# Up-projection weights of a conv-FFN: store fewer split operands, split three of seven anew in each chunk

## The chip, the cores and the metric

The kernel runs on one core of one Trainium2 chip. TensorE multiplies; VectorE, ScalarE and GpSimd (POOL in the profile) prepare operands and take results out of PSUM; SyncE (SP) issues nearly all DMAs from one in-order queue. The metric is device time in microseconds, the median of the runs.

## The reference

One layer of a hybrid decoder: a mixing sub-layer (dilated window attention and gated linear attention) and a feed-forward sub-layer, for 2048 prompt tokens and 64 sample tokens. The change is in the second half, the feed-forward part, and in what leads to it:

```python
def conv_ffn(xn, conv_buf, w_up, conv_w, conv_b, w_down):
    T = xn.shape[1]
    up = xn @ w_up
    g, u = jnp.split(up, 2, axis=-1)
    gp = jnp.concatenate([conv_buf.astype(g.dtype), g], axis=1)
    c = conv_b + sum(conv_w[j] * gp[:, j:j + T] for j in range(CONV_W))
    h = jax.nn.gelu(c, approximate=False) * u
    return h @ w_down, gp[:, T:]
...
    x = x + rmsnorm(mixed, g_post_mix)
    f, conv_new = conv_ffn(rmsnorm(x, g_pre_ffn), conv_buf, w_up, conv_w, conv_b, w_down)
    x = x + rmsnorm(f, g_post_ffn)
```

The model width is 1024, the hidden width 2816 (22 tiles of 128), all in float32.

## The kernel before, in words

**Precision.** Every float32 operand is split into a high part (ScalarE rounds it, line 68) and a low part (operand minus high part, on GpSimd or VectorE, line 71; the argument "p" or "v" chooses). A product then takes three matmuls: high x high, high x low, low x high.

**Chunks.** The 2112 tokens are cut into four chunks of 528, each of two halves of 264. `tail` first runs the output projection (`wo`, with its inputs from `wo_x` and its normalisation in `post`) for all four chunks, and then `ffn` four times. `ffn` walks over pairs of hidden tiles, 11 pairs a chunk, in the groups of `FG` (sizes in tiles). For each pair it computes the gate product, the convolution and gelu, then the up product (`strassen` with z = 0 and z = 1), multiplies the two and splits the result into hh and hl. After a group, `down` multiplies the group's hidden tiles with the down weights and adds to `acc`, eight output tiles m.

**Seven products.** `strassen` computes a 2 x 2 block product (two hidden tiles by two token halves, over the two halves of the model width) with seven products instead of eight. Each product is 12 matmuls of 264 columns: 4 model tiles by 3 parts. Its seven weight operands come from the generator `wsrc`, and the seven input operands from `ffn_x`. Results leave PSUM by ScalarE copies (lines 1381, 1383) and VectorE adds (line 1379), in between further products that add to the same bank.

**Where the operands come from.** In chunk 0, `wsrc` loads two raw weight tiles of 512 KB (`wraw`, tile wr), forms three sums on VectorE (four operations, lines 1363 to 1366), splits all seven operands, low parts alternately on GpSimd and VectorE, and stores all seven in DRAM (d_wst, line 1372). Chunks 1 to 3 load the seven, 512 KB each (line 1357). The down weights go the same way: raw and split in chunk 0, stored in d_wdst (line 1407), loaded in the later chunks (line 1402).

**Order and buffers.** The order of work on each engine and on the DMA queue comes from a scheduler with a timeline of its own, starting from the order of the program text. Split weights pass through a ring of eight slots ("w") in the feed-forward part. Raw weights have two buffers, raw input tiles five. The final step of a chunk (`final`, normalisation and output) is a generator `pend`, which the next chunk advances by four steps after each `strassen`, and drains at the end of its first group (in chunk 0, of its second).

```python
        for i, src in enumerate((g0[:, lo], g0[:, hi], t3[:, 1], g1[:, lo], t3[:, 0], t3[:, 2], g1[:, hi])):
            t = self.slot("w", [128, 2, 512], F32R, "ws")
            t4 = t.rearrange("p a (k c) -> p a k c", k=4)
            self.split(t4[:, 0], t4[:, 1], src, "pvpvpvp"[i])
            yield t4
            nc.sync.dma_start(wt[i], t.bitcast(F32))
```

Of the kernel before, what the change touches and what calls it, by code (L numbers as in the profile page):

```python
# [18 lines left out]
KT = 8  # L19
# [8 lines left out]
H = 264  # L28
FCH = tuple((2 * H * c, H, H) for c in range(4))
FG = (2, 4, 4, 4, 4, 4)  # L30

# [5 lines left out]
class Layer:  # L37
# [1131 lines left out]
    def raw(self):  # L1169
        return self.xpool.tile([128, 2 * H], F32, name=self.n("br"), tag="raw", bufs=5)  # L1170

    def wraw(self, src, nk=8):
        raw = self.xpool.tile([128, 8, 128], F32, name=self.n("wr"), tag="wr", bufs=2)
        self.nc.sync.dma_start(raw[:, :nk], src.rearrange("p (k c) -> p k c", k=nk))
        return raw
# [24 lines left out]
    def tail(self):  # L1200
        nc, a = self.nc, self.a
        with ExitStack() as ctx:
            self.xpool = self.pool(ctx, "tx", side="right")
            self.gk = "h"
            self.slots, self.scnt = {}, {}
            self.bx = [self.xpool.tile([128, 2 * H], F32, name=self.n("bx"), tag="px", bufs=3) for _ in range(3)]
            p = self.npool = self.pool(ctx, "tn")
            self.psum = self.pool(ctx, "tps", bass.MemoryType.PSUM)
            posts = []
            with ExitStack() as c1:  # L1210
                self.spool = self.pool(c1, "tw")
                self.ring("w", 4, 12)
                self.ring("hl", 8, 16)
                self.wow = []
                for _ in self.wo_x(0):
                    pass
                for c in range(4):
                    nxt = self.wo_x(c + 1) if c < 3 else iter(())
# [24 lines left out]
            for _ in pend:  # L1243
                pass

    def wo_x(self, c):
# [5 lines left out]
        for k in self.WORD:  # L1252
# [37 lines left out]
    def post(self, c, mot, ssq):  # L1290
# [7 lines left out]
        for m in range(KT):  # L1298
            r = self.bx.pop(0) if self.bx else self.xpool.tile([128, w], F32, name=self.n("bx"), tag="px", bufs=3)
            nc.sync.dma_start(r, a["xn"][:, m, t0:t0 + w])  # L1300
# [14 lines left out]
    def ffn_x(self, c):  # L1315
# [35 lines left out]
    def wsrc(self, c, f, z):  # L1351
        nc, a = self.nc, self.a
        wt = a["wst"][f // 2, z]
        if c:
            for i in range(7):
                t = self.slot("w", [128, 2, 512], F32R, "ws")
                nc.sync.dma_start(t.bitcast(F32), wt[i])
                yield t.rearrange("p a (k c) -> p a k c", k=4)
            return
        g0, g1 = (self.wraw(a["wu"][2 * (f + j) + z]) for j in range(2))  # L1360
        t3 = self.spool.tile([128, 3, 4, 128], F32, name=self.n("wt"), tag="wt", bufs=1)
        lo, hi = slice(0, 4), slice(4, 8)
        nc.vector.tensor_tensor(t3[:, 0], g0[:, lo], g1[:, lo], op=ALU.subtract)
        nc.vector.tensor_tensor(g1[:, lo], g1[:, lo], g1[:, hi], op=ALU.add)
        nc.vector.tensor_tensor(t3[:, 1], g1[:, lo], g0[:, lo], op=ALU.subtract)
        nc.vector.tensor_tensor(t3[:, 2], g0[:, hi], t3[:, 1], op=ALU.subtract)
        for i, src in enumerate((g0[:, lo], g0[:, hi], t3[:, 1], g1[:, lo], t3[:, 0], t3[:, 2], g1[:, hi])):
# [4 lines left out]
            nc.sync.dma_start(wt[i], t.bitcast(F32))  # L1372

    def strassen(self, c, f, z, xs, o11, o12, o21, o22):
# [3 lines left out]
        p1, u2, u4 = (self.spool.tile([128, H], F32, name=self.n(n), tag=n, bufs=2) for n in ("p1", "u2", "u4"))  # L1378
        add = lambda o, x, y: nc.vector.tensor_tensor(o, x, y[:, :H], op=ALU.add)
        for i, (bank, new, ev) in enumerate((  # L1380
# [8 lines left out]
            for k in range(4):  # L1389
                xh, xl = xs[self.PROD[i]][k]  # L1390
                for j, (ww, xx) in enumerate(((0, xh), (0, xl), (1, xh))):
                    self.lastmm = nc.tensor.matmul(bank[:, :H], w[:, ww, k, :], xx, start=new and k == 0 and j == 0,  # L1392
                                                   stop=k == 3 and j == 2, skip_group_check=not new)
            ev()
        next(ws, None)

    def down_w(self, c, gi, m, f0, G):
        nc, a = self.nc, self.a
        t = self.slot("w", [128, 2, 512], F32R, "ws")
        dst = a["wdst"][gi, m][:, :, :G * 128]  # L1400
        if c:
            nc.sync.dma_start(t[:, :, :G * 128].bitcast(F32), dst)
        else:
            raw = self.wraw(a["wd"][m, :, f0 * 128:(f0 + G) * 128], G)
            t4 = t.rearrange("p a (k c) -> p a k c", k=4)
            self.split(t4[:, 0, :G], t4[:, 1, :G], raw[:, :G])
            nc.sync.dma_start(dst, t[:, :, :G * 128].bitcast(F32))
        return tuple(t[:, j].rearrange("p (k c) -> p k c", k=4) for j in range(2))

    def down(self, c, gi, f0, G, hs, acc, last):  # L1410
        nc = self.nc
        for m in range(KT):
            w = self.down_w(c, gi, m, f0, G)
            ps = [self.bank("pfd"), self.bank("pfd")]
# [15 lines left out]
    def ffn(self, c, xs, pend):  # L1430
# [7 lines left out]
        down = None  # L1438
        steps = lambda n: [pend and next(pend, None) for _ in range(n)]
        for gi, G in enumerate(FG):  # L1440
            hs = []
            for pi in range(G // 2):
                gts = [sp.tile([128, w + 2], F32, name=self.n("gt"), tag="gt", bufs=3) for _ in range(2)]
                for j in range(2):
                    nc.vector.tensor_copy(gts[j][:, 0:2], halo[:, f + j, :])
                self.strassen(c, f, 0, xs, *(gts[j][:, 2 + z * H:2 + z * H + H] for j in range(2) for z in range(2)))
                steps(4)
                if down is not None:
# [24 lines left out]
                ups = [sp.tile([128, w], F32, name=self.n("up"), tag="up", bufs=2) for _ in range(2)]  # L1473
                self.strassen(c, f, 1, xs, *(ups[j][:, z * H:z * H + H] for j in range(2) for z in range(2)))
                for j in range(2):
                    nc.vector.tensor_tensor(cts[j], cts[j], ups[j], op=ALU.mult)
# [5 lines left out]
                steps(4)  # L1482
            if gi == (c == 0) and pend is not None:
# [17 lines left out]
    def ffn_end(self, c, acc, hs, f0, G):  # L1501
        nc, a = self.nc, self.a
        wds = [self.down_w(c, len(FG) - 1, m, f0, G) for m in range(KT)]
        t0 = FCH[c][0]
# [25 lines left out]
    def final(self, c, acc, ssq, s0, w, fx=None):  # L1530
# [7 lines left out]
        for m in range(KT):  # L1538
# [4 lines left out]
            else:  # L1543
                r = self.xpool.tile([128, 2 * H], F32, name=self.n("fx"), tag="px", bufs=3)
                nc.sync.dma_start(r[:, :w], a["x1"][:, m, t0:t0 + w])
# [159 lines left out]
def pack_inputs(inp):  # L1705
# [14 lines left out]
    def vt(cols):  # L1720
# [30 lines left out]
SCRATCH = {**{"%s%d" % (t, i): (128, 2048) for t in ("qh", "ql", "kh", "kl") for i in range(4)}, "awd": (3, 96, 128),  # L1751
           "wst": (NF // 2, 2, 7, 128, 2, 512), "wdst": (len(FG), KT, 128, 2, 512),
           "mixa": (128, 4, S), "mixb": (128, 4, T), "x1": (128, KT, T), "rs1": (128, T), "rs2": (128, T)}
# [41 lines left out]
```

## Time and profile before

| | us |
|---|---|
| median of 3 runs | 3118.58 (3111.11 to 3120.32) |
| profiled execution | 3115.91, span 3114.1 |
| busy in the span: TensorE matmul | 2821.7 (91%) |
| VectorE | 1735.3 (56%) |
| ScalarE | 1125.8 (36%) |
| GpSimd | 1148.7 (37%) |
| mean granted TensorE clock | 0.953 |
| DMA | 717.08 MB, mean 230 GB/s |

Busy times are unions of the instructions' intervals. In rows by stage, each engine has its busy time and its count of instructions, then come the granted clock of TensorE, the mean busy share of 16 DMA engines and the GB/s moved. In rows of waits stand the total in us, the number of times and the longest. In groups of instructions stand the busy time, the mean duration in ns, and the idle time of the engine ahead of them with its releasers.

### The profile page before, as it was taken

To read this page: it belongs to the slowest core of one execution; us is meant where nothing else is said; L and a number is where in the kernel's file an instruction comes from. 1 tells how busy PE (TensorE), PEld (TensorE's weight loads), DVE (VectorE), ACT (ScalarE), POOL (GpSimd) and SP (SyncE) were. 2 spreads that over 40 slices of the span, in tenths; PEclk is the share of its full clock that TensorE was granted. 3 is DMA by queue.
4 is the path that set the end of the run, shared out by engine and by line. 5 is a ranking of instruction groups with operands and counts; after the bars stand their busy time and mean duration, and the time that the engine had idled before them with its cause. 6 is when DMAs were issued, how large, how long until landed. Compare 5 with 4: busy or idle time off the path is not lost. (4 is left out here: it accounts for less than half of the span.)

```text
span 3114.1 us, 57988 instructions
## 1 busy us (share of the span) xinstructions
PE 2821.7 (91%) x22255; PEld 2605.2 (84%) x22255; DVE 1735.3 (56%) x4085; ACT 1125.8 (36%) x2633; POOL 1148.7 (37%) x926
## 2 busy tenths in 40 slices
PE   7998899999898996997778788899999999999997
PEld 5777698887677775996777777899998999999997
DVE  7677855443255565357866666643348333563435
ACT  5545443333276664443433333321123121231112
POOL 5656544334325545534444444520114011231002
PEclk9999999999999988997888999999999999999998
DMA  5323326798966653434777777897888888798875
GB/s 168 119 79 117 111 63 204 260 337 323 279 141 144 134 124 100 148 118 156 284 270 278 283 278 273 286 348 275 298 306 291 325 303 304 272 334 299 294 273 213
DMA packets 291861, 717.08 MB, mean 230 GB/s; under 512 B 30049, under 2 KB 105729, under 8 KB 286465
## 3 DMA queue, kind: packets, MB, share of 16 engines
q1 hardware_dynamic: 286528, 684.14, 63.8%
q0 software_dynamic: 5056, 29.24, 4.1%
q8 instruction: 176, 2.88, 0.4%
q14 instruction: 101, 0.82, 0.1%
HBM read 554.51 MB, written 158.75 MB: 229 GB/s over the span
## 5 line engine op out<-in xcount | busy, mean ns | idle before, releaser
L90 PE MATMUL pfd<-hh,ws 128*128 128x264 f32 x2816 | 479.9, 288 | 36.4 <-ACT ws L68 9.4
L71 POOL TENSOR_TENSOR hl<-ct,hh 128x528 fp32r<-128x528 f32 x88 | 133.6, 1531 | 825.9 <-ACT hh L68 814.6
L90 PEld LDWEIGHTS pfd<-hh,ws 128*128 128x128 f32 x2816 | 402.3, 191 | 42.1 <-ACT hh L68 11.5
L1392 PE MATMUL pfe<-xh,ws 128*128 128x264 f32 x1408 | 304.1, 295 | 59.2 <-ACT ws L68 25.0
L71 POOL TENSOR_TENSOR wl<-wr,wh 128x1024 fp32r<-128x1024 f32 x102 | 253.9, 2496 | 209.4 <-ACT wh L68 170.6
L1392 PE MATMUL pfa<-xh,ws 128*128 128x264 f32 x1408 | 303.7, 295 | 14.3 <-ACT ws L68 5.3
L1392 PEld LDWEIGHTS pfe<-xh,ws 128*128 128x128 f32 x1408 | 239.7, 195 | 69.3 <-ACT ws L68 28.3
L90 PE MATMUL pfd<-hl,ws 128*128 128x264 f32 x1408 | 296.8, 287 | 0.2 <-POOL hl L71 0.2
L1392 PE MATMUL pfd<-xh,ws 128*128 128x264 f32 x1408 | 292.0, 288 | 2.2 <-ACT xh L68 1.4
L1392 PEld LDWEIGHTS pfa<-xh,ws 128*128 128x128 f32 x1408 | 239.8, 196 | 21.6 <-ACT ws L68 6.7
L364 PE MATMUL pv<-wh,xh 128*128 128x256 f32 (+1 forms) x816 | 238.9, 293 | 8.6 <-DVE th L655 4.4
L1423 DVE TENSOR_TENSOR acc<-acc,pfd 128x264 f32<-128x264 f32 x304 | 116.6, 424 | 220.6 <-PE pfd L90 220.5
L1392 PEld LDWEIGHTS pfd<-xh,ws 128*128 128x128 f32 x1408 | 234.9, 192 | 3.0 <-ACT xh L68 1.7
L364 PE MATMUL pv<-wl,xh 128*128 128x256 f32 (+1 forms) x816 | 236.0, 289 | 0.0
L364 PE MATMUL pv<-wh,xl 128*128 128x256 f32 (+1 forms) x816 | 235.6, 289 | 0.0
L90 PEld LDWEIGHTS pfd<-hl,ws 128*128 128x128 f32 x1408 | 224.7, 191 | 0.7 <-POOL hl L71 0.7
L1609 ACT ACTIVATE ass<-ass,aml 128x256 f32<-128x256 f32 (+1 forms) x384 | 174.5, 456 | 119.1 <-DVE aml L1604 116.7
L1392 PE MATMUL pfa<-xl,ws 128*128 128x264 f32 x704 | 206.3, 293 | 1.3 <-POOL xl L71 1.3
L1392 PE MATMUL pfe<-xl,ws 128*128 128x264 f32 x704 | 205.3, 292 | 0.0
L71 POOL TENSOR_TENSOR ws<-wr,ws 128x512 fp32r<-128x512 f32 (+1 forms) x92 | 128.3, 1396 | 206.2 <-ACT ws L68 163.0
L1392 PE MATMUL pfd<-xl,ws 128*128 128x264 f32 x704 | 203.1, 288 | 1.0 <-POOL xl L71 1.0
L1604 DVE CUSTOM_DVE_ANT_0 ass<-pas,amask 128x256 f32<-128x256 f32 (+1 forms) x384 | 129.0, 363 | 104.7 <-PE pas L1603 95.7
(330 smaller groups left out, 7236.3 us busy)
## 6 DMA issues: line engine op xcount, KB each, us to landing
ws<-d_wst SPq DMA_DIRECT2D x462, 512.0 KB
d_wst<-ws SPq DMA_DIRECT2D x154, 512.0 KB
ws<-d_wdst SPq DMA_DIRECT2D x120, 512.0 KB
wr<-in_wt SPq DMA_DIRECT2D x95, 512.0 KB
wr<-in_wu SPq DMA_DIRECT2D x44, 512.0 KB
d_wdst<-ws SPq DMA_DIRECT2D x40, 512.0 KB
skp<-in_ckt SPq DMA_DIRECT2D x16, 1024.0 KB
svp<-in_cv SPq DMA_DIRECT2D x16, 1024.0 KB
```

What stands on the lines that cost most here:

```text
L71: (nc.gpsimd if lo_eng == "p" else nc.vector).tensor_tensor(lo, src, hi.bitcast(F32), op=ALU.subtract)
L90: mm = nc.tensor.matmul(o, ww[:, k, :], xx[:, s0:s0 + n], start=(k == order[0] and i == 0), stop=(k == order[-1] and i == 2))
L364: mm = nc.tensor.matmul(ps[:m, :256], x[:, t0:t0 + m], w[:, k % 4, :], start=(k == 0 and i == 0), stop=(k == KT - 1 and i == 2))
L1392: self.lastmm = nc.tensor.matmul(bank[:, :H], w[:, ww, k, :], xx, start=new and k == 0 and j == 0, stop=k == 3 and j == 2, skip_group_chec ...
L1423: nc.vector.tensor_tensor(acc[m][:, s0:s0 + n], acc[m][:, s0:s0 + n], pz, op=ALU.add)
L1604: nc.vector.tensor_tensor_reduce(ssb[:, sc:sc + nk], ps[:, sc:sc + nk], L.amk[:, self.pat, 256 - nk:256], scale=1.0, scalar=3e38, op0=ALU. ...
L1609: nc.scalar.activation(ssb[:, sc:sc + nk], ssb[:, sc:sc + nk], AF.Exp, bias=self.ml[:, idx, h:h + 1], scale=-1.0, accum_out=self.ml[:, idx ...
```

## The change

- `wsrc`: in chunk 0 six of the seven low parts are made on VectorE and the seventh on GpSimd, and only the four operands 2 to 5 are stored. In chunks 1 to 3 these four are loaded, and operands 0, 1 and 6 are split anew from raw tiles (one whole, of the other the second half).
- `down_w`: the down weights are loaded raw and split in every chunk, low parts on GpSimd; nothing is stored.
- Low parts of the hidden tiles, of the output projection's inputs after chunk 0, and of one of the input operands go from GpSimd to VectorE.
- Buffers: raw weights 4 instead of 2, raw input tiles 4 instead of 5, tiles px 4 instead of 3, the scratch tile wt 2 instead of 1, p1 and u4 1 instead of 2; the weight ring has as many slots as before, of which two, not four, lie in the pool that is there before the feed-forward part.
- `FG` is (4, 4, 4, 4, 2, 4) instead of (2, 4, 4, 4, 4, 4). The steps of `pend` are taken one after each second product instead of four after each `strassen`.

```diff
-FG = (2, 4, 4, 4, 4, 4)
+FG = (4, 4, 4, 4, 2, 4)
...
-        return self.xpool.tile([128, 2 * H], F32, name=self.n("br"), tag="raw", bufs=5)
-
-    def wraw(self, src, nk=8):
-        raw = self.xpool.tile([128, 8, 128], F32, name=self.n("wr"), tag="wr", bufs=2)
-        self.nc.sync.dma_start(raw[:, :nk], src.rearrange("p (k c) -> p k c", k=nk))
+        return self.xpool.tile([128, 2 * H], F32, name=self.n("br"), tag="raw", bufs=4)
+
+    def wraw(self, src, nk=8, k0=0):
+        raw = self.xpool.tile([128, 8, 128], F32, name=self.n("wr"), tag="wr", bufs=4)
+        self.nc.sync.dma_start(raw[:, k0:nk], src.rearrange("p (k c) -> p k c", k=nk)[:, k0:])
...
-                self.ring("w", 4, 12)
+                self.ring("w", 2, 14)
...
-            self.ring("w", 4, 4)
+            self.ring("w", 2, 6)
...
-            self.split(hi, lo, r, ("p" if k % 2 else "v") if c else self.SB["xe"][k])
+            self.split(hi, lo, r, "v" if c else self.SB["xe"][k])
...
-            self.split(hi, lo, r, "p" if i % 2 else "v")
+            self.split(hi, lo, r, "p" if i else "v")
...
-            put(r0, 1, ("b11", k), ("t1", k))
+            put(r0, 0, ("b11", k), ("t1", k))
...
-        if c:
-            for i in range(7):
-                t = self.slot("w", [128, 2, 512], F32R, "ws")
-                nc.sync.dma_start(t.bitcast(F32), wt[i])
-                yield t.rearrange("p a (k c) -> p a k c", k=4)
-            return
...
+        g0, g1 = (self.wraw(a["wu"][2 * (f + j) + z], k0=4 * (j and c > 0)) for j in range(2))
+        src = [g0[:, lo], g0[:, hi], None, None, None, None, g1[:, hi]]
+        if c == 0:
+            t3 = self.spool.tile([128, 3, 4, 128], F32, name=self.n("wt"), tag="wt", bufs=2)
...
+            src[2:6] = t3[:, 1], g1[:, lo], t3[:, 0], t3[:, 2]
+        for i in range(7):
             t = self.slot("w", [128, 2, 512], F32R, "ws")
             t4 = t.rearrange("p a (k c) -> p a k c", k=4)
-            self.split(t4[:, 0], t4[:, 1], src, "pvpvpvp"[i])
+            if src[i] is None:
+                nc.sync.dma_start(t.bitcast(F32), wt[i - 2])
+            else:
+                self.split(t4[:, 0], t4[:, 1], src[i], "p" if i == 6 else "v")
             yield t4
-            nc.sync.dma_start(wt[i], t.bitcast(F32))
...
+            if c == 0 and 2 <= i < 6:
+                nc.sync.dma_start(wt[i - 2], t.bitcast(F32))
...
+            if i % 2 == 0:
+                pend and next(pend, None)
...
+    def down_w(self, m, f0, G):
+        raw = self.wraw(self.a["wd"][m, :, f0 * 128:(f0 + G) * 128], G)
+        t4 = self.slot("w", [128, 2, 512], F32R, "ws").rearrange("p a (k c) -> p a k c", k=4)
+        self.split(t4[:, 0, :G], t4[:, 1, :G], raw[:, :G])
+        return t4[:, 0], t4[:, 1]
...
-                    self.split(hi, lo, cts[j], "p")
+                    self.split(hi, lo, cts[j], "v")
```

More of the change, by code (lines that the diff above doesn't have):

```diff
@@ L1205, in tail @@
             self.slots, self.scnt = {}, {}
-            self.bx = [self.xpool.tile([128, 2 * H], F32, name=self.n("bx"), tag="px", bufs=3) for _ in range(3)]
+            self.bx = [self.xpool.tile([128, 2 * H], F32, name=self.n("bx"), tag="px", bufs=4) for _ in range(4)]
             p = self.npool = self.pool(ctx, "tn")
@@ L1298, in post @@
         for m in range(KT):
-            r = self.bx.pop(0) if self.bx else self.xpool.tile([128, w], F32, name=self.n("bx"), tag="px", bufs=3)
+            r = self.bx.pop(0) if self.bx else self.xpool.tile([128, w], F32, name=self.n("bx"), tag="px", bufs=4)
             nc.sync.dma_start(r, a["xn"][:, m, t0:t0 + w])
@@ L1353, in wsrc, with strassen @@
         wt = a["wst"][f // 2, z]
-        if c:
-            for i in range(7):
-                t = self.slot("w", [128, 2, 512], F32R, "ws")
-                nc.sync.dma_start(t.bitcast(F32), wt[i])
-                yield t.rearrange("p a (k c) -> p a k c", k=4)
-            return
-        g0, g1 = (self.wraw(a["wu"][2 * (f + j) + z]) for j in range(2))
-        t3 = self.spool.tile([128, 3, 4, 128], F32, name=self.n("wt"), tag="wt", bufs=1)
-        lo, hi = slice(0, 4), slice(4, 8)
[L1363 to L1367, printed above, removed]
+        lo, hi = slice(0, 4), slice(4, 8)
+        g0, g1 = (self.wraw(a["wu"][2 * (f + j) + z], k0=4 * (j and c > 0)) for j in range(2))
+        src = [g0[:, lo], g0[:, hi], None, None, None, None, g1[:, hi]]
+        if c == 0:
+            t3 = self.spool.tile([128, 3, 4, 128], F32, name=self.n("wt"), tag="wt", bufs=2)
+            nc.vector.tensor_tensor(t3[:, 0], g0[:, lo], g1[:, lo], op=ALU.subtract)
+            nc.vector.tensor_tensor(g1[:, lo], g1[:, lo], g1[:, hi], op=ALU.add)
+            nc.vector.tensor_tensor(t3[:, 1], g1[:, lo], g0[:, lo], op=ALU.subtract)
+            nc.vector.tensor_tensor(t3[:, 2], g0[:, hi], t3[:, 1], op=ALU.subtract)
+            src[2:6] = t3[:, 1], g1[:, lo], t3[:, 0], t3[:, 2]
+        for i in range(7):
             t = self.slot("w", [128, 2, 512], F32R, "ws")
             t4 = t.rearrange("p a (k c) -> p a k c", k=4)
-            self.split(t4[:, 0], t4[:, 1], src, "pvpvpvp"[i])
+            if src[i] is None:
+                nc.sync.dma_start(t.bitcast(F32), wt[i - 2])
+            else:
+                self.split(t4[:, 0], t4[:, 1], src[i], "p" if i == 6 else "v")
             yield t4
-            nc.sync.dma_start(wt[i], t.bitcast(F32))
-    def strassen(self, c, f, z, xs, o11, o12, o21, o22):
+            if c == 0 and 2 <= i < 6:
+                nc.sync.dma_start(wt[i - 2], t.bitcast(F32))
+    def strassen(self, c, f, z, xs, pend, o11, o12, o21, o22):
         nc = self.nc
@@ L1377, in strassen @@
         pa, pb, pd, pe = (self.bank(n) for n in ("pfa", "pfb", "pfd", "pfe"))
-        p1, u2, u4 = (self.spool.tile([128, H], F32, name=self.n(n), tag=n, bufs=2) for n in ("p1", "u2", "u4"))
+        p1, u2, u4 = (self.spool.tile([128, H], F32, name=self.n(n), tag=n, bufs=b) for n, b in (("p1", 1), ("u2", 2), ("u4", 1)))
         add = lambda o, x, y: nc.vector.tensor_tensor(o, x, y[:, :H], op=ALU.add)
@@ L1394, in strassen @@
             ev()
+            if i % 2 == 0:
+                pend and next(pend, None)
         next(ws, None)
[L1397 to L1408, printed above, removed]
+    def down_w(self, m, f0, G):
[3 more added lines that the diff above has]
+        return t4[:, 0], t4[:, 1]
     def down(self, c, gi, f0, G, hs, acc, last):
@@ L1412, in down @@
         for m in range(KT):
-            w = self.down_w(c, gi, m, f0, G)
+            w = self.down_w(m, f0, G)
             ps = [self.bank("pfd"), self.bank("pfd")]
@@ L1438, in ffn @@
         down = None
-        steps = lambda n: [pend and next(pend, None) for _ in range(n)]
         for gi, G in enumerate(FG):
@@ L1445, in ffn @@
                     nc.vector.tensor_copy(gts[j][:, 0:2], halo[:, f + j, :])
-                self.strassen(c, f, 0, xs, *(gts[j][:, 2 + z * H:2 + z * H + H] for j in range(2) for z in range(2)))
-                steps(4)
+                self.strassen(c, f, 0, xs, pend, *(gts[j][:, 2 + z * H:2 + z * H + H] for j in range(2) for z in range(2)))
                 if down is not None:
@@ L1473, in ffn @@
                 ups = [sp.tile([128, w], F32, name=self.n("up"), tag="up", bufs=2) for _ in range(2)]
-                self.strassen(c, f, 1, xs, *(ups[j][:, z * H:z * H + H] for j in range(2) for z in range(2)))
+                self.strassen(c, f, 1, xs, pend, *(ups[j][:, z * H:z * H + H] for j in range(2) for z in range(2)))
                 for j in range(2):
@@ L1478, in ffn @@
                     lo = self.t528("hl", "hhl", 8, F32R)
-                    self.split(hi, lo, cts[j], "p")
+                    self.split(hi, lo, cts[j], "v")
                     hs.append((hi, lo))
                 f += 2
-                steps(4)
             if gi == (c == 0) and pend is not None:
@@ L1502, in ffn_end @@
         nc, a = self.nc, self.a
-        wds = [self.down_w(c, len(FG) - 1, m, f0, G) for m in range(KT)]
+        wds = [self.down_w(m, f0, G) for m in range(KT)]
         t0 = FCH[c][0]
@@ L1543, in final @@
             else:
-                r = self.xpool.tile([128, 2 * H], F32, name=self.n("fx"), tag="px", bufs=3)
+                r = self.xpool.tile([128, 2 * H], F32, name=self.n("fx"), tag="px", bufs=4)
                 nc.sync.dma_start(r[:, :w], a["x1"][:, m, t0:t0 + w])
@@ L1751 @@
 SCRATCH = {**{"%s%d" % (t, i): (128, 2048) for t in ("qh", "ql", "kh", "kl") for i in range(4)}, "awd": (3, 96, 128),
-           "wst": (NF // 2, 2, 7, 128, 2, 512), "wdst": (len(FG), KT, 128, 2, 512),
+           "wst": (NF // 2, 2, 4, 128, 2, 512),
            "mixa": (128, 4, S), "mixb": (128, 4, T), "x1": (128, KT, T), "rs1": (128, T), "rs2": (128, T)}
```

## The prediction

> **What bounds the kernel now.** I read the page's slices first, then busy time by stage, then the waits of TensorE and of the DMA queue inside the stage that stands out, then its groups of instructions. The slices (each 77.9 us):
>
> ```profile
> PE   7998899999898996997778788899999999999997
> ...
> DMA  5323326798966653434777777897888888798875
> ```
>
> The feed-forward part is the right half. TensorE stands at 7 to 8 in slices 18 to 22 (its first chunk) and mostly at 9 from slice 23 on (the other three), with DMA high throughout. By chunk, roughly:
>
> ```profile
> core 0: us, PE busy (x) PEld busy (x) DVE busy (x) ACT busy (x) POOL busy (x), PEclk, DMA share, GB/s
> 1468.00:1975.00 507.00, 401.97 (x2831) 379.81 (x2829) 353.06 (x521) 194.15 (x350) 235.96 (x160) 0.91 0.76 274
> 1975.00:2352.00 377.00, 365.60 (x2943) 364.11 (x2943) 171.71 (x349) 82.35 (x153) 70.18 (x48) 0.98 0.85 301
> 2352.00:2722.00 370.00, 363.19 (x2946) 361.23 (x2945) 175.13 (x352) 83.72 (x153) 70.59 (x49) 0.99 0.85 302
> 2722.00:3114.00 392.00, 366.62 (x2983) 363.72 (x2981) 191.12 (x489) 82.21 (x160) 72.65 (x58) 0.98 0.80 282
> ```
>
> A chunk has 11 pairs x 2 x 7 products x 12 matmuls = 1848, and 22 x 8 x 2 x 3 = 1056 of the down-projection: 2904. Their undisturbed pace stands in the chain of waits:
>
> ```profile
> 2087.39 23.32 PE pfd L90 x192
> ```
>
> That is 0.1215 us each, 353 us a chunk. So chunks 1 and 2 carry 17 to 24 us of loss, chunk 3 (with the tail) some 39, and chunk 0 about 154. The prize is in chunk 0. What it waits for there, on TensorE and then on the DMA queue (SP):
>
> ```profile
> PE pfe L1392 <- ACT ws L68: 20.7, 13, 3.6
> PE pfe L1392 <- DVE ws L71: 19.6, 13, 2.4
> ...
> PE pfe L1392 <- DVE u L1379: 12.6, 14, 0.9
> PE pfb L1392 <- DVE ws L71: 7.9, 7, 2.6
> SPq L1372 <- POOL ws L71: 101.7, 38, 6.6
> SPq L1407 <- POOL ws L71: 85.9, 37, 5.3
> SPq L1372 <- DVE ws L71: 67.2, 28, 10.2
> ```
>
> TensorE waits for split weights (ws). The one SP queue spends 255 us of the 507 at the stores of those split weights (L1372, L1407), mostly until GpSimd has made the low part, and the next raw loads (L1174), two tiles deep, stand behind them. The transfers are heavy too:
>
> ```profile
> ws<-d_wst SPq DMA_DIRECT2D x462, 512.0 KB
> d_wst<-ws SPq DMA_DIRECT2D x154, 512.0 KB
> ws<-d_wdst SPq DMA_DIRECT2D x120, 512.0 KB
> ...
> wr<-in_wu SPq DMA_DIRECT2D x44, 512.0 KB
> d_wdst<-ws SPq DMA_DIRECT2D x40, 512.0 KB
> ...
> wr<-in_wd SPq DMA_DIRECT2D x40, 256.0 KB
> ```
>
> Chunk 0 moves 154 + 44 + 40 pieces of 512 KB, 40 of 256 KB, and the small last pieces of the group of two: 138 MB, which is the 274 GB/s of its row. At the best rate of the table, 302 GB/s, that alone would be 458 us, above TensorE's 353.
>
> **The change: transfers.** Chunk 0 stores 88 operands instead of 154 and no down weights: 46 + 23 + 12 = 81 MB, 267 us at 302 GB/s. The later chunks load 88 stored operands, 22 x 768 KB of raw and 12 MB of down weights: 75 MB instead of 104. So DMA drops under TensorE everywhere, and the SP queue loses its stores behind GpSimd. With four raw tiles the loads of the next half-pair start while this one is split. SP's order stays: a raw load can stand behind a stored-operand load that waits for a slot.
>
> **The change: engines in chunk 0.** Three of seven low parts move from GpSimd to VectorE (22 x 3 = 66), and 22 low parts of the hidden tiles. The groups of VectorE, GpSimd and ScalarE in that stage, then three rows of the timelines:
>
> ```profile
> L71 DVE TENSOR_TENSOR ws<-wr,ws 128x512 fp32r<-128x512 f32 x42 | 51.2, 1220 | 22.5 <-ACT ws L68 22.4
> L1466 DVE SCALAR_TENSOR_TENSOR ct<-gt,c_cw,ct 128x528 f32<-128x528 f32 x44 | 41.1, 954 | 2.3 <-ACT ct L1457 2.1
> L1476 DVE TENSOR_TENSOR ct<-ct,up 128x528 f32<-128x528 f32 x22 | 27.9, 1270 | 0.4
> L1365 DVE TENSOR_TENSOR wt<-wr,wr 128x512 f32<-128x512 f32 x20 | 27.6, 1382 | 0.3
> ...
> L1366 DVE TENSOR_TENSOR wt<-wr,wt 128x512 f32<-128x512 f32 x20 | 27.3, 1364 | 0.0
> L1364 DVE TENSOR_TENSOR wr<-wr 128x512 f32<-128x512 f32 x20 | 21.4, 1070 | 0.9 <-DVE wt L1363 0.4
> L1363 DVE TENSOR_TENSOR wt<-wr,wr 128x512 f32<-128x512 f32 x20 | 18.8, 940 | 1.3 <-DMA wr<-in_wu 1.3
> ...
> L1379 DVE TENSOR_TENSOR u<-u,pfe 128x264 f32<-128x264 f32 x22 | 9.4, 428 | 37.0 <-ACT u L1383 37.0
> ...
> L71 POOL TENSOR_TENSOR ws<-wr,ws 128x512 fp32r<-128x512 f32 x77 | 109.1, 1418 | 191.1 <-ACT ws L68 148.0 <-DMA wr<-in_wu 20.2 <-DMA d_wst<-ws 10.9
> L71 POOL TENSOR_TENSOR ws<-wt,ws 128x512 fp32r<-128x512 f32 x42 | 69.2, 1653 | 37.6 <-ACT ws L68 33.6 <-issue 1.3 <-PE pfa L1392 1.3
> L71 POOL TENSOR_TENSOR hl<-ct,hh 128x528 fp32r<-128x528 f32 x22 | 35.3, 1609 | 24.2 <-ACT hh L68 24.2
> ...
> L68 ACT ACTIVATE ws<-wr 128x512 fp32r<-128x512 f32 x120 | 72.6, 626 | 109.9 <-DMA wr<-in_wu 46.3 <-DMA wr<-in_wd 38.8 <-issue 9.1
> ...
> 1683.08 0.68 DVE L1363 TENSOR_TENSOR wt<-wr,wr 128x512 f32<-128x512 f32 x1
> ...
> 1689.14 1.78 DVE L71 TENSOR_TENSOR ws<-wr,ws 128x512 fp32r<-128x512 f32 x1
> ...
> 1688.62 1.75 POOL L71 TENSOR_TENSOR hl<-ct,hh 128x528 fp32r<-128x528 f32 x1
> ```
>
> The same VectorE operation takes 0.68 us alone and 1.78 while GpSimd runs; an add that reads PSUM (L1379) keeps 0.43. GpSimd's busy time falls from 236 us to about 106: 22 + 40 weight splits at 1.42 are 88, the rest small pieces and the next chunk's input. VectorE gains 66 x 0.68 + 22 x 0.71 = 61 us. What it loses to GpSimd now is the groups' means less their time alone (0.68 for 512 columns; 0.71 and 0.76 for the 528 of L1476 and L1466), by their counts: 42 x 0.54 + 44 x 0.19 + 22 x 0.56 + 20 x (0.70 + 0.68 + 0.39 + 0.26) = 84 us, 0.36 us per us of GpSimd. After: 106 x 0.36, and a third more because more VectorE work is exposed: 51. So VectorE comes to 353 - 84 + 61 + 51 = 381 us, a little over TensorE. Neither engine reaches 100% here; VectorE's densest stretches with TensorE running are these, with the interior of a late chunk and the projection before for comparison:
>
> ```profile
> 1360.00:1442.00 82.00, 82.00 (x682) 82.00 (x682) 50.23 (x77) 31.10 (x68) 30.68 (x17) 1.00 0.37 122
> 2330.00:2400.00 70.00, 62.89 (x496) 61.62 (x495) 57.28 (x95) 23.47 (x40) 36.00 (x25) 0.97 0.85 303
> 2400.00:2700.00 300.00, 299.74 (x2449) 299.10 (x2447) 116.11 (x259) 60.83 (x114) 33.43 (x23) 1.00 0.85 302
> ```
>
> At the boundary (second row) VectorE is at 82% with TensorE at 90%. Over a whole chunk, with low parts that can be made up to eight slots ahead, I take 92%: 381 / 0.92 = 414 us. Gain in chunk 0: 93. The ends are 82% (465 us, gain 42) and chunk 1's 377 us (gain 130). The clock's 0.91 should return towards the 0.98 of the next row, and lies inside that gain. ScalarE's 194 us keep room; its row waits 85 us for raw loads now, the lateness that the four tiles are to take away.
>
> **The change: chunks 1 to 3.** They now split three operands of seven and all down weights. Per chunk: ScalarE 66 + 48 more high parts at 0.63 (82 us become about 154); GpSimd 70 less 33 for the hidden tiles' low parts and 6 for half the input's, plus 22 x 1.42 = 31 and some 65 for the down weights: 127; VectorE 172 + 44 x 0.68 + 22 x 0.71 + 3 + (127 - 70) x 0.36 = 241, 65% of the chunk. The transfer hidden before becomes a chain of raw load, high part, low part, whose cover is the eight slots (eight products of 1.47 us) and the four raw tiles. If it stays covered, what is paid is the wait of TensorE for VectorE's adds. In chunk 0, at 70% VectorE, that is the 12.6 us row; in the interior of late chunks, at 39%, TensorE runs 299.74 of 300. I interpolate about 10 us, add 5 for low parts that come late, and take off 4.5: the wait below sits once in a late chunk, and the new group order gives the final step of the previous chunk four products' steps more to finish ahead of it.
>
> ```profile
> PE pfd L90 <- DMA out_o_y<-acc: 4.4, 1, 4.4
> ```
>
> So +10 a chunk, +30 in all. Bounds: -3 a chunk (adds stay on time, that wait goes) to +25 (a whole chunk at the boundary's 90%: 353 / 0.90 = 393).
>
> **Edits at the edges.** Four raw input tiles instead of five make the next chunk's input more serial; its cover is the last group's 23.32 us on TensorE, and its first low part leaves GpSimd. The single p1 and u4 buffers are read five products before they are written again (7 us). The output projection's low parts go to VectorE under a TensorE that is fully busy (82.00 of 82). Only two, not four, early weight slots exist before the feed-forward part starts. In the tail the last eight down weights are split: GpSimd's 1.42 us against 12 matmuls of 1.46. I take +5 for all, between -5 and +15.
>
> **Sum.** -93 + 30 + 5 = -58. The profiled execution took 3115.9 us (span 3114.1), 2.7 under the median of 3118.6; on the median the sum gives 3060.6, said as 3060.
>
> **The rivals.**
> - *VectorE paces everything.* Chunk 0 only comes to 435 (gain 72; 88% VectorE), the late chunks pay 25 each, the edges 5: +8, 3127. For it: VectorE is the one engine over 90% by my sum. Against it: the eight slots of lead.
> - *The late chunks inherit chunk 0's lateness* (slower). The place: a VectorE low part of a raw operand waits for its load and high part, and TensorE's adds stand behind it on VectorE. If the three of seven operands are as late as now in chunk 0, 154 x 3/7 = 66 us a chunk: +198 - 93 + 5 = +110, 3229. It decides from 30 us a chunk on. For it: the 26 waits at pfe on ACT or DVE ws. Against: those stood behind 2 raw tiles and 138 MB.
> - *The port empties.* If VectorE's operations fall back to 0.68 wherever GpSimd is quiet, chunk 0 is TensorE's again, at chunk 1's 377 us, the late chunks -3 each: -130 - 9 + 0 = -139, 2980. For it: without GpSimd's share VectorE needs 353 - 84 + 61 = 330 us in chunk 0, under TensorE's 353. Against it: 106 us of GpSimd remain there, and 57 come in each late chunk. The Trainium skill, "SBUF — State Buffer", section "Who interferes with whom", says that a VectorE instruction with two SBUF inputs and a GpSimd one that reads SBUF share a read interface under an exclusive lock; the two rows and the unchanged 0.43 of the PSUM add agree, and by that rule alone VectorE's two-input work and GpSimd's work in chunk 0 must fit in sequence, which favours this rival.
> - *No effect.* The stores were not what held the raw loads, and TensorE waits as before: chunk 0 gains 30, the late chunks take it back: 3118.
>
> **How the numbers follow.** A difference under 0.3% (9.4 us) is about what a measurement of this kernel can't tell from none. Forecast 0.60 (own range 3015 to 3100), VectorE paces 0.11, late chunks late 0.13, port empties 0.10, no effect 0.06. The range reaches down to the port case and up past the pacing case: 2980 to 3135. Faster is the forecast, the port case and a little of the pacing case: 0.71; slower the late case and some of the pacing case: 0.16; same 0.13.
>
> **What would show it.** Right: chunk 0 at 400 to 430 us, DMA share there 0.6 or less, no SP waits on POOL ws; GpSimd near 106 us and VectorE near 381 in it; late chunks 380 to 390 with VectorE about 241 and DMA near 200 GB/s. Wrong: VectorE ws (L71) or ACT ws among TensorE's longest waits in a late chunk, waits on u above 15 us a chunk, or chunk 0 with TensorE still under 80%.

## The result and the profile after

The changed kernel takes 2997.7 us, the kernel before 3118.1 us on the same chip: a ratio of 0.9617 (95% interval 0.9600 to 0.9635), 120 us less. The forecast was 3060 us, in a range of 2980 to 3135: the direction and the stage were right, the size was half of what came.

The page of the changed kernel, slices of 74.9 us, TensorE and DMA, and its DMA issues:

```profile
PE   6989989999979899699789998999999999999997
...
DMA  5323325599776773432666656766567665676654
...
ws<-d_wst SPq DMA_DIRECT2D x264, 512.0 KB
wr<-in_wu SPq DMA_DIRECT2D x110, 512.0 KB
...
d_wst<-ws SPq DMA_DIRECT2D x88, 512.0 KB
wr<-in_wd SPq DMA_DIRECT2D x160, 256.0 KB
wr<-in_wu SPq DMA_DIRECT2D x66, 256.0 KB
```

The trough in the first chunk is nearly gone, and DMA stands at 5 to 7 where it stood at 7 to 9. By stage, this time cut exactly, from the first matmul of a chunk to the first of the next (the last one ends with the span); the kernel before, then the changed one:

```profile
1442.00:1990.00 548.00, 421.19 (x2912) 395.40 (x2911) 389.43 (x567) 210.91 (x378) 260.88 (x177) 0.89 0.76 271
1990.00:2360.00 370.00, 363.90 (x2958) 362.87 (x2958) 167.70 (x344) 79.71 (x147) 65.42 (x45) 0.99 0.85 302
2360.00:2727.00 367.00, 360.19 (x2922) 358.23 (x2920) 172.08 (x349) 81.52 (x149) 67.52 (x46) 0.99 0.85 303
2727.00:3114.00 387.00, 361.62 (x2942) 358.72 (x2940) 186.75 (x483) 80.92 (x158) 67.80 (x55) 0.98 0.80 282
```

```profile
1440.00:1852.00 412.00, 374.94 (x2950) 367.53 (x2951) 359.46 (x655) 204.41 (x375) 119.54 (x80) 0.95 0.63 225
1852.00:2229.00 377.00, 366.39 (x2923) 364.23 (x2922) 234.65 (x423) 145.50 (x267) 131.13 (x91) 0.97 0.65 219
2229.00:2602.00 373.00, 360.80 (x2915) 359.08 (x2914) 232.71 (x417) 142.08 (x262) 126.99 (x88) 0.99 0.65 220
2602.00:2994.00 392.00, 365.17 (x2942) 363.33 (x2940) 258.93 (x553) 144.68 (x272) 132.15 (x103) 0.96 0.60 203
```

Columns: stage, length, then busy time and count of TensorE, its weight loads, VectorE, ScalarE and GpSimd, the granted clock, DMA share and GB/s. To a tenth, from the first matmuls: chunk 0 went from 548.0 to 412.1 us (-135.9), chunks 1 to 3 from 370.2, 367.0 and 386.7 to 376.8, 373.7 and 392.0 (+6.6, +6.8, +5.3), and all before chunk 0 is 2.5 us shorter. That is the -119.7 us of the spans. Of chunk 0's 136 us, 90 are idle time of TensorE (length less busy time: 126.8 us before, 37.2 after), and 46 are busy time: the chunk's matmuls take 374.9 us instead of 421.2, with the granted clock at 0.95 instead of 0.89.

What TensorE and the DMA queue wait for in the changed kernel's chunk 0:

```profile
PE pfb L1393 <- ACT xh L68: 8.8, 3, 5.0
PE pb L134 <- DVE rcy L108: 7.5, 2, 6.1
PE pfe L1393 <- ACT ws L68: 5.1, 1, 5.1
PE pfe L1393 <- DVE u L1380: 2.3, 4, 1.1
...
SPq L1174 <- POOL ws L71: 98.8, 66, 4.6
SPq L1373 <- DVE ws L71: 61.2, 43, 8.9
```

The waits for split weights, 48 us in the three rows shown of before, have gone to 5 in the same rows; what is left is mostly the start of the chunk (xh, rcy). The queue now waits mostly at the raw loads (L1174), for a free one of the four tiles: it is ahead of the work.

### The profile page after: what moved, and what is told of

It reads as the page before. It is cut to its first block, busy times and chain, and to the rows that moved or that the text cites. A ratio compares the mean times of both kernels' runs of the same rounds, so it can differ in the third digit from the quotient of the medians.

```text
span 2994.4 us, 58590 instructions
## 1 busy us (share of the span) xinstructions
PE 2781.3 (93%) x22255; PEld 2583.1 (86%) x22255; DVE 1909.8 (64%) x4399; ACT 1308.5 (44%) x2975; POOL 1176.1 (39%) x954
## 4 chain that ended last, share of the span: by engine, by line
PE 69%; DVE 16%; DMA 7%; issue 3%; POOL 3%; ACT 2%; SPq 1%; DVEq 0%; POOLq 0%; ACTq 0%
PE pfd L90 14%; PE pfe L1393 8%; PE pfa L1393 8%; PE pfd L1393 7%; PE pv L364 7%; PE pq L90 6%; PE pbo L90 5%; PE pfb L1393 4%; PE pas L1596 2%; PE pao L1635 2%; DMA awb<-d_awd 2%; PE pat L1618 2%; DVE xl L71 1%; DVE acc L1541 1%; DVE ktb L725 1%
## 5 line engine op out<-in xcount | busy, mean ns | idle before, releaser
L71 POOL TENSOR_TENSOR ws<-wr,ws 128x512 fp32r<-128x512 f32 (+1 forms) x280 | 397.0, 1433 | 930.1 <-ACT ws L68 868.1
L68 ACT ACTIVATE ws<-wr 128x512 fp32r<-128x512 f32 (+1 forms) x478 | 291.8, 616 | 331.3 <-PE pfd L90 161.1
L1393 PE MATMUL pfe<-xh,ws 128*128 128x264 f32 x1408 | 295.1, 290 | 19.0 <-DVE u L1380 13.2
L1393 PE MATMUL pfa<-xh,ws 128*128 128x264 f32 x1408 | 296.2, 290 | 8.8 <-DVE ws L71 3.8
L71 DVE TENSOR_TENSOR ws<-wr,ws 128x512 fp32r<-128x512 f32 x198 | 137.5, 695 | 120.1 <-ACT ws L68 116.1
```

Of the source, the lines that this page charges most:

```text
L68: nc.scalar.activation(hi, src, AF.Copy)
L71: (nc.gpsimd if lo_eng == "p" else nc.vector).tensor_tensor(lo, src, hi.bitcast(F32), op=ALU.subtract)
```

## The experiments

The question after the result was why chunk 0 gained 136 us and not 93. Theory A: transfers, that is raw loads late behind stores, and 138 MB. Theory B: the port, that is VectorE's and GpSimd's operations meeting. Chunk 0's length tells more than the medians, which also carry the later chunks; it is read from one profiled execution of each kernel, from first matmul to first matmul.

| kernel | median us (ratio to before, 95%) | chunk 0 us |
|---|---|---|
| before | 3118.1 | 548.0 |
| before, 4 raw tiles | 3035.4 (0.9738; 0.9713 to 0.9763) | 461.5 |
| before, low parts on VectorE | 3078.1 (0.9872; 0.9837 to 0.9907) | 505.9 |
| before, both of these | 3022.7 (0.9696; 0.9666 to 0.9726) | 448.8 |
| changed | 2997.7 (0.9617; 0.9600 to 0.9635) | 412.1 |
| changed, 2 raw tiles | 3053.4 (0.9781; 0.9751 to 0.9811) | 452.0 |
| changed, low parts as before | 3030.7 (0.9716; 0.9687 to 0.9744) | 441.2 |
| changed, stores as before | 3052.4 (0.9776; 0.9740 to 0.9811) | 442.5 |

**Two raw tiles in the changed kernel.**

```diff
-        raw = self.xpool.tile([128, 8, 128], F32, name=self.n("wr"), tag="wr", bufs=4)
+        raw = self.xpool.tile([128, 8, 128], F32, name=self.n("wr"), tag="wr", bufs=2)
```

> The changed kernel with two raw weight tiles instead of four. Theory A (transfers: chunk 0 was held by raw loads that came late behind stores on the one queue, and by 138 MB): most of the gain of chunk 0 needs the deeper prefetch, so 40 to 80 us of the 136 us gained in chunk 0 are lost, 3040 to 3080 us, and the late chunks, which now split anew, lose too. Theory B (port: chunk 0 was held by VectorE's and GpSimd's operations meeting): 10 to 20 us lost, about 3010 us.

Chunk 0 lost 40 us, the low end of what theory A said; 8 more were lost ahead of chunk 0 and 9 in the late chunks. The group of ScalarE's high parts in chunk 0 shows it in its idle time and releasers (a row names three at most): of this kernel, of the changed kernel, and of the kernel before with four tiles:

```profile
L68 ACT ACTIVATE ws<-wr 128x512 fp32r<-128x512 f32 x129 | 79.2, 628 | 100.7 <-DMA wr<-in_wu 48.3 <-DMA wr<-in_wd 36.1 <-DVE wr L1360 5.9
```

```profile
L68 ACT ACTIVATE ws<-wr 128x512 fp32r<-128x512 f32 x128 | 79.5, 629 | 61.0 <-PE pfe L1393 21.7 <-PE pfd L90 18.3 <-DMA wr<-in_wu 4.9
```

```profile
L68 ACT ACTIVATE ws<-wr 128x512 fp32r<-128x512 f32 x126 | 75.2, 623 | 47.9 <-issue 13.9 <-DMA wr<-in_wu 13.1 <-PE pfe L1392 7.6
```

With two tiles ScalarE waits 84 us for raw loads, as it did before the change (85). With four, the rows name 5 and 13 us of waits for up weights; with the down weights, which the rows no longer name, the trace has 8 and 20.

**Four raw tiles in the kernel before, and nothing else.**

```diff
-        raw = self.xpool.tile([128, 8, 128], F32, name=self.n("wr"), tag="wr", bufs=2)
+        raw = self.xpool.tile([128, 8, 128], F32, name=self.n("wr"), tag="wr", bufs=4)
```

> The kernel before with four raw weight tiles instead of two and nothing else. If the raw loads' lateness by itself held chunk 0, 30 to 45 us go (3075 to 3090), as taking the four tiles away from the changed kernel cost 40 us in chunk 0. If the stores on the same queue (255 us of waits at them) and the 138 MB hold the loads back in any case, under 15 us go (3103 to 3118).

This one number alone gives 83 us, where the whole change gives 120; I expected 45 at most. With stores and bytes unchanged the raw loads do come early, and the queue still waits 185 us at the stores in the three rows of before:

```profile
SPq L1372 <- POOL ws L71: 87.1, 58, 4.7
SPq L1407 <- POOL ws L71: 54.4, 33, 9.5
SPq L1372 <- DVE ws L71: 43.7, 24, 5.1
```

What holds the stage then is taken up below, with its row.

**Low parts of chunk 0, taken back and done alone.** In the changed kernel:

```diff
-                self.split(t4[:, 0], t4[:, 1], src[i], "p" if i == 6 else "v")
+                self.split(t4[:, 0], t4[:, 1], src[i], "pvpvpvp"[i] if c == 0 else "p" if i == 6 else "v")
...
-                    self.split(hi, lo, cts[j], "v")
+                    self.split(hi, lo, cts[j], "v" if c else "p")
```

> The changed kernel with chunk 0's low parts where they were before: weights alternately on GpSimd and VectorE, hidden tiles on GpSimd; chunks 1 to 3 unchanged. Theory A (transfers): within 10 us of the changed kernel, 2998 to 3008 us. Theory B (port): VectorE's weight operations meet GpSimd again (30 of 43 did before, 3 of 66 after), chunk 0 grows by 40 to 80 us, 3040 to 3075 us.

In the kernel before:

```diff
-            self.split(t4[:, 0], t4[:, 1], src, "pvpvpvp"[i])
+            self.split(t4[:, 0], t4[:, 1], src, "p" if i == 6 else "v")
...
-                    self.split(hi, lo, cts[j], "p")
+                    self.split(hi, lo, cts[j], "p" if c else "v")
```

> The kernel before with only chunk 0's low parts moved as in the change (six of seven weights and the hidden tiles on VectorE). Theory A (transfers): within 15 us of before, 3103 to 3125 us. Theory B (port): 40 to 80 us of chunk 0's loss go, 3040 to 3080 us.

29 us lost and 42 us gained: theory B holds too, below its range of 40 to 80 us in the first and at its lower end in the second. VectorE's groups in chunk 0, of the changed kernel and of this first experiment:

```profile
L71 DVE TENSOR_TENSOR ws<-wr,ws 128x512 fp32r<-128x512 f32 x66 | 46.1, 700 | 6.0 <-ACT ws L68 5.6
...
L1460 DVE SCALAR_TENSOR_TENSOR ct<-gt,c_cw,ct 128x528 f32<-128x528 f32 x44 | 43.4, 994 | 2.2 <-ACT ct L1451 2.0
...
L1470 DVE TENSOR_TENSOR ct<-ct,up 128x528 f32<-128x528 f32 x22 | 19.9, 903 | 0.3
```

```profile
L1460 DVE SCALAR_TENSOR_TENSOR ct<-gt,c_cw,ct 128x528 f32<-128x528 f32 x44 | 52.4, 1208 | 2.3 <-ACT ct L1451 2.0
L71 DVE TENSOR_TENSOR ws<-wr,ws 128x512 fp32r<-128x512 f32 x45 | 39.8, 885 | 6.4 <-ACT ws L68 6.2
...
L1470 DVE TENSOR_TENSOR ct<-ct,up 128x528 f32<-128x528 f32 x22 | 22.7, 1034 | 0.4
```

The same subtraction takes 0.70 us where GpSimd has 120 us of work in the stage, and 0.89 where it has 247. The two edits do a second thing: a low part that took GpSimd 1.4 to 1.7 us takes VectorE 0.7, so that it is ready earlier, and no run parts this from the meeting. In the first experiment, though, none of TensorE's waits in chunk 0 names a GpSimd operation, and the largest in total, 18.1 us where the changed kernel has 2.3, is for VectorE's adds:

```profile
PE pfe L1393 <- DVE u L1380: 18.1, 11, 3.7
```

**The stores of before, added to the changed kernel's chunk 0.** 66 operands and 48 down-weight tiles go to a scratch tensor as well:

```diff
-            if c == 0 and 2 <= i < 6:
-                nc.sync.dma_start(wt[i - 2], t.bitcast(F32))
+            if c == 0:
+                dst = wt[i - 2] if 2 <= i < 6 else a["wst2"][f // 2, z, min(i, 2)]
+                nc.sync.dma_start(dst, t.bitcast(F32))
...
+        if c == 0:
+            nc = self.nc
+            nc.sync.dma_start(self.a["wdst"][f0 // 2, m][:, :, :G * 128], t[:, :, :G * 128].bitcast(F32))
```

> The changed kernel, in chunk 0 with the stores of before in addition (66 operands of 512 KB and the 48 down-weight tiles, 58 MB, which nothing reads). Theory A (transfers): chunk 0 again has 138 MB, 458 us at 302 GB/s against 412 us now, so 45 to 70 us are lost, 3040 to 3070 us. Theory B (port): under 15 us lost, 3000 to 3013 us.

The whole lost 55 us, as theory A said, but chunk 0 only 30 of the 45 to 70 it was to lose. Chunk 1 lost 15 more (391.7 us), 14.4 of them in one wait of TensorE for the high part of its input, and 6 were lost ahead of chunk 0.

**Both small edits in the kernel before** (four raw tiles, and chunk 0's low parts on VectorE), everything stored and loaded as before:

> The kernel before with four raw weight tiles and chunk 0's low parts on VectorE; everything is stored and loaded as before. If chunk 0 has three limits (raw loads late, VectorE and GpSimd meeting, and 138 MB of transfers), two are gone and the transfers remain: 138 to 145 MB at the 315 to 328 GB/s of the runs with four raw tiles, 435 to 450 us in chunk 0, late chunks as before (370): 3005 to 3020 us. If the transfers are no limit: 412 us, 2982 us.

Chunk 0 by stage in three kernels: before with four raw tiles; the changed one with the stores; before with both edits:

```profile
1444.00:1905.00 461.00, 394.51 (x2928) 379.23 (x2927) 366.27 (x556) 199.53 (x372) 251.53 (x172) 0.92 0.85 316
```

```profile
1446.00:1888.00 442.00, 383.59 (x2929) 368.83 (x2929) 348.52 (x646) 200.13 (x373) 114.17 (x80) 0.95 0.87 328
```

```profile
1448.00:1897.00 449.00, 388.06 (x2952) 375.28 (x2952) 352.68 (x645) 200.97 (x372) 126.38 (x87) 0.94 0.88 328
```

Here is the third limit, the transfers. As soon as the loads come early, the 138 MB (some 145 to 147 with what else moves) run at 316 to 328 GB/s with the DMA engines busy for 85 to 88% of the time; before, it was 271. The last two kernels take 442.5 and 448.8 us, with VectorE at 79%. The rate is read over the same stretch, so it does not show by itself that the transfers set its length. What speaks for it is what ScalarE waits for in the changed kernel with the stores:

```profile
L68 ACT ACTIVATE ws<-wr 128x512 fp32r<-128x512 f32 x128 | 76.8, 624 | 46.0 <-DMA wr<-in_wd 12.8 <-DMA wr<-in_wu 12.1 <-issue 5.9
L68 ACT ACTIVATE ws<-wt 128x512 fp32r<-128x512 f32 x66 | 40.8, 627 | 45.2 <-DMA d_wst<-ws 21.2 <-DVE wt L1362 8.2 <-DVE wt L1361 5.9
```

That is 25 us for raw loads and 21 for stores that had yet to leave their slot; in the trace of the changed kernel the same groups have 8 and 4. And either half of the added stores alone costs chunk 0 nothing: 406.4 us with the 66 operands (308 GB/s) and 412.5 with the down weights (280 GB/s), both in runs shown further down. Whether it is the rate or the slots that wait for their stores, no run parts. Two edits without fewer stores end 25 us above the change, at 3022.7 us just over the 3005 to 3020 expected, with chunk 0 inside its range.

**The group order and the steps as before**, in the changed kernel (the last two lines stand at two places, once for each `strassen`):

```diff
-FG = (4, 4, 4, 4, 2, 4)
+FG = (2, 4, 4, 4, 4, 4)
...
-            if i % 2 == 0:
-                pend and next(pend, None)
...
+                for _ in range(4):
+                    pend and next(pend, None)
```

> The changed kernel with the group order (2, 4, 4, 4, 4, 4) and with the steps of the previous chunk's final stage taken four after each seven products, as before. If the order carries part of what three undone parts leave unexplained in chunk 0 (136 us against 40 + 29 + 30), chunk 0 grows by 15 to 35 us and each late chunk by the 4.5 us wait for the output store: 3025 to 3045 us. If it carries nothing but that wait: 3003 to 3013 us.

3003.8 us, ratio 0.9636 (0.9614 to 0.9659): 415.6 us in chunk 0, 377.0 and 378.2 after it. At most a few us lie in the order; it is no fourth cause.

**The late chunks.** Four edits looked for their 5 to 7 us. The first loads all seven operands again, from a chunk 0 that stores them:

```diff
...
-        src = [g0[:, lo], g0[:, hi], None, None, None, None, g1[:, hi]]
+        src = [None] * 7
...
+            src = [g0[:, lo], g0[:, hi], None, None, None, None, g1[:, hi]]
...
```

> The changed kernel, but chunk 0 stores all seven operands and the late chunks load all seven (down weights split anew as in the change). If splitting three operands anew is what costs the late chunks their 5 to 7 us each, they come back to 367 to 370 us, against 15 to 20 us more in chunk 0 for 35 MB of stores: 2990 to 3005 us. If the late chunks' cost is the down weights' or the boundary's, they stay at 374 to 377 and the whole is slower: 3010 to 3020 us.

3000.5 us (0.9624; 0.9597 to 0.9651). Chunk 0 did not grow (406.4 us, at 308 GB/s), where 15 to 20 us more were expected, and the late chunks did not come back (378.6, 374.1): the three operands split anew cost nothing that shows.

The second has one input operand's low part on GpSimd, as before:

```diff
-            self.split(hi, lo, r, "p" if i else "v")
+            self.split(hi, lo, r, "p" if i % 2 else "v")
...
-            put(r0, 0, ("b11", k), ("t1", k))
+            put(r0, 1, ("b11", k), ("t1", k))
```

> The changed kernel with the low part of one input operand (r0) on GpSimd again, as before: four operations for each chunk, all at the boundary of two chunks, where VectorE is dense. If VectorE's load there is what costs the late chunks 5 to 7 us, each boundary gains 2 to 5 us: 2983 to 2993 us. If GpSimd, which splits down weights there, becomes late instead, nothing or a loss: 2995 to 3010 us.

The third has the hidden tiles' low parts of the late chunks on GpSimd:

```diff
-                    self.split(hi, lo, cts[j], "v")
+                    self.split(hi, lo, cts[j], "p" if c else "v")
```

> The changed kernel with the hidden tiles' low parts of chunks 1 to 3 on GpSimd again. Taking operands 0, 1 and 6 off the late chunks' splitting did not bring them back (378, 374 us against 370, 367 before). If VectorE's load at the boundaries costs them 5 to 7 us each, VectorE loses some 16 us a chunk and the late chunks gain 2 to 4 us each: 2986 to 2992 us. If GpSimd's operations there cost as much by meeting VectorE's, no difference: 2994 to 3002 us.

The fourth stores the down weights in chunk 0 and loads them later:

```diff
-    def down_w(self, m, f0, G):
+    def down_w(self, m, f0, G, c=3):
+        if c:
+            t = self.slot("w", [128, 2, 512], F32R, "ws")
+            self.nc.sync.dma_start(t[:, :, :G * 128].bitcast(F32), self.a["wdst"][f0 // 2, m][:, :, :G * 128])
+            return tuple(t[:, j].rearrange("p (k c) -> p k c", k=4) for j in range(2))
...
+        self.nc.sync.dma_start(self.a["wdst"][f0 // 2, m][:, :, :G * 128], t[:, :, :G * 128].bitcast(F32))
```

> The changed kernel with the down weights stored in chunk 0 and loaded in the late chunks; operands 0, 1 and 6 are still split anew. Chunk 0 stays under the transfer limit (104 MB): 408 to 416 us. If the down weights' splitting on GpSimd at the boundaries costs the late chunks their 5 to 7 us each, they come back to 370: 2978 to 2988 us. If not, 2994 to 3004 us.

The third and the fourth together:

> The changed kernel with both: down weights stored and loaded, and the late chunks' hidden low parts on GpSimd. If VectorE at the boundaries is the cost, it is at its lowest here: 2974 to 2986 us. If the late chunks' cost lies in the boundary's order or transfers, 2994 to 3004 us.

| changed kernel, with | median us (ratio to before, 95%) | chunks 1, 2 us |
|---|---|---|
| (nothing) | 2997.7 (0.9617; 0.9600 to 0.9635) | 376.8, 373.7 |
| input low part on GpSimd | 2998.3 (0.9620; 0.9593 to 0.9647) | 376.8, 373.1 |
| hidden low parts on GpSimd | 3003.1 (0.9629; 0.9606 to 0.9652) | 377.1, 377.2 |
| down weights loaded | 2993.2 (0.9601; 0.9581 to 0.9621) | 371.3, 372.0 |
| the last two | 2998.8 (0.9618; 0.9596 to 0.9639) | 370.3, 374.0 |

None of the four gave the late chunks' cost back as a whole: the first, second and third came out as if VectorE's load and the three operands did not matter, the third even 1 us above its range, and the fourth between its two ranges; the last two together came out in the range that was given for no gain. By the interiors the cost sits at the boundaries. The interior of two late chunks of the changed kernel, and 80 us across the end of chunk 1, first changed, then before:

```profile
1900.00:2200.00 300.00, 300.00 (x2465) 300.00 (x2464) 166.61 (x317) 115.38 (x214) 87.56 (x63) 1.00 0.64 214
2270.00:2570.00 300.00, 300.00 (x2454) 300.00 (x2454) 170.11 (x316) 114.28 (x211) 90.08 (x65) 0.99 0.64 216
...
2189.00:2269.00 80.00, 68.21 (x518) 66.77 (x517) 67.08 (x108) 33.81 (x60) 43.90 (x28) 0.94 0.69 236
```

```profile
2324.00:2404.00 80.00, 72.89 (x571) 71.62 (x570) 64.73 (x108) 27.56 (x46) 40.00 (x27) 0.96 0.83 297
```

In the interior TensorE never stops, with VectorE at 56%; across the boundary it does 53 matmuls fewer in the same 80 us (518 against 571; 6.4 us at 0.1215). The same cut gives 77 fewer at the end of chunk 2 (523 against 600), but 6 more at the end of chunk 0 (482 against 476). Loading the down weights gives back 5.5 us in chunk 1 and 1.7 in chunk 2, and chunk 3 loses 1.8, each from one execution. That is within what the same code varied: in the four kernels whose late chunks are those of before (before, four raw tiles, low parts on VectorE, both), chunk 1 took 370.2, 375.3, 366.3 and 372.1 us. The three late chunks together took 1121 to 1131 us in these four, 1143 in the changed kernel and 1137 with the down weights loaded. The median of the last is the lowest of all, but its interval overlaps that of the change: a better version is not shown. What part of the boundary's cost is the splitting of the down weights, and what the rest is, stays open.

## Why the prediction was right or wrong

**Right.** The prize was chunk 0; DMA there fell to 0.63 of the time (0.6 or less was said) and GpSimd to 107 to 120 us (106 was said); ScalarE had room; the late chunks paid +6.6, +6.8 and +5.3 where +10 was taken, with VectorE at 233 to 235 us in chunks 1 and 2 (241 was said); what lies ahead of chunk 0 became 2.5 us shorter where the edges were to cost +5. One sign named for it did not come: the queue still waits for GpSimd's low parts (98.8 us), now at the raw loads, where it is ahead.

**The step that failed is "381 / 0.92 = 414 us. Gain in chunk 0: 93".** It measured 136. The forecast's window left out 26 us at the head and 15 at the end of chunk 0 (the slices, too, stay at 7 to 8 as far as slice 25, counted from 0, not 22); the same cut of the changed kernel is this row:

```profile
1466.00:1837.00 371.00, 352.23 (x2815) 348.17 (x2815) 320.94 (x590) 187.91 (x346) 107.42 (x73) 0.97 0.64 227
```

371 us, not 414. (That chunk 0 whole takes 412 is a coincidence: its forecast on the same footing would have been some 455.)

The mis-sized term is VectorE's work: 321 us, not 381. Of the 84 us that it lost to GpSimd some 24 are left, where 51 were expected. The changed kernel's groups have 2 x 66 splits at 0.70 us, 44 convolution steps at 0.99 and 22 products at 0.90: over their time alone that is 2.6 + 10 + 4 us, some 24 with the sums and the hidden low parts. I had scaled the loss by GpSimd's busy time. But it matters which operations meet. Chunk 0's low parts on GpSimd were made side by side with VectorE's own low parts and sums of the same operands; most of what is left on GpSimd belongs to the down weights. Of 43 low parts of raw operands that VectorE made in chunk 0 before, 30 overlapped a GpSimd operation by over 0.1 us, afterwards 3 of 66 (13 of 45 with the low parts put back). Splits that follow one another closely also start every 0.60 us, though each is recorded with 0.68, and I had added 88 operations at 0.68 and 0.71: in that cut 39 us of VectorE's records overlap one another, in the forecast's 24. The two make up some 42 of the 60 us; the rest of it is not worked out.

The second half of the step, that VectorE would pace the chunk at 92%, was wrong in kind. The interior of chunk 0, changed and before:

```profile
1552.00:1852.00 300.00, 292.25 (x2386) 290.37 (x2385) 258.53 (x467) 146.66 (x268) 91.64 (x63) 1.00 0.63 225
```

```profile
1552.00:1852.00 300.00, 238.22 (x1704) 226.72 (x1703) 201.08 (x289) 105.66 (x187) 135.56 (x93) 0.91 0.76 275
```

TensorE runs for 97% of it beside VectorE at 86%. So the 90% beside 82% that I took from a boundary does not carry over to a busy VectorE elsewhere; that it comes from the boundary's chain of dependent steps is my reading, not shown.

**The rivals.** The emptied port was right for chunk 0 (371 us in that cut, 377 said) and wrong for the late chunks, which got no better. That it came so near is in part luck: it had no term for the raw tiles either, and with two of them chunk 0 stays at 452 us though the low parts are on VectorE. The Trainium skill, "SBUF — State Buffer", section "Who interferes with whom", says that a VectorE instruction with two SBUF inputs contends with a GpSimd one that reads SBUF, and that the shared ports are an exclusive lock; 0.70 against 0.89 us for the same subtraction agrees. The late chunks did not inherit the lateness: one wait of 3.8 us for VectorE's low part heads the list of chunk 1, and no wait for a split weight is longer. VectorE does not pace the interiors; across the end of chunk 0 it is busy for 72.6 of 80 us beside TensorE's 67.6, and whether it paces there is not shown.

**The cause as I told it** was the stores on the queue and the bytes. The largest single part was one that I gave no term of its own, the second pair of raw tiles: 87 us of chunk 0 alone. With four tiles alone the queue kept 185 of its 255 us at the stores while chunk 0 lost 87: most of that waiting cost nothing once loads could be issued further ahead. And I took 302 GB/s for the best rate, where 328 was to be had.

**The wait taken off the late chunks** (4.5 us for the output store) is gone from their lists, and the added waits for VectorE's adds (u) are 0.2, 5.6 and 5.2 us, below the 10 a chunk that were interpolated; they come in one or two waits a chunk, not spread over it.

## What to carry to other kernels

A stage can stand under several limits of nearly the same height. Here, with the other two lifted, buffer depth gives 452 us, the low parts on GpSimd 441, and the stores 442 (449 in the kernel before with the other two edits), and with none of them 412. Lifted from 548, buffer depth alone gives 87 and the low parts alone 42, but both together 99, not 129; the stores alone were not lifted. So price each limit with the others gone, and look early for one that a number of buffers lifts: a queue that waits long at stores may only mean that the loads behind it have nowhere to go. And when work moves between two engines whose operations lengthen each other, ask which operations met, not how long the engine was busy.

## What the runs showed of the hardware

The mixed traffic of loads and stores of 512 KB reached 328 GB/s over 442 us, with the DMA engines busy for 87%, while chunks 1 and 2 of the kernel before, loads only for the most part, ran at 302 to 303 at 85%.
